# Sixteen weight chunks of a float32 decoder block: the low part built by a negative copy and an adding transfer

## The chip, the cores and the metric

The kernel runs on one core of a Trainium2 chip. The engines are TensorE (PE in the profile; its weight loads are the row PEld), VectorE (DVE), ScalarE (ACT), GpSimd (POOL) and SyncE (SP, which here issues nearly all transfers). The metric is the device time of one launch in microseconds. A span is the time from the first to the last instruction of one profiled execution.

## The reference

A decoder block on a sequence of 512 tokens of width 1024, in float32: a first gated feed-forward part, a token mixer (causal pooling beside dilated window attention, gated and merged), a second gated feed-forward part, and a final norm. The change is in the second feed-forward part only.

```python
def swiglu(u, w_in, w_out):
    a, b = jnp.split(u @ w_in, 2, axis=-1)
    return (jax.nn.silu(a) * b) @ w_out
...
u = modulate(rmsnorm(h, g_norm_ffn2[l]), sh3, sc3)
h = h + 0.5 * gt3 * swiglu(u, w_ffn2_in[l], w_ffn2_out[l])
return rmsnorm(h, g_final)
```

The hidden width is 2816, which is 22 tiles of 128.

## The kernel before, in words

**Float32 by three products.** Every float32 operand is cut into a high part of type fp32r and a low part, the rest. A product is then three matmuls into the same PSUM bank: high weight by high activation, high weight by low activation, low weight by high activation (`mm3`, lines 360 to 362; lines 745 to 747 in `product`).

**The weight pipeline.** Weights come from HBM in chunks, mostly 128x1024 float32 (512 KB), in an order that the planner `plan` writes down once (`self.order`). `fetch` issues the load of a chunk from SP (line 245) into a raw buffer as soon as one is free; three buffers are always there (`raw`), and up to four more (`X` in the profile) in part of the second feed-forward part. `split_hi` lets ScalarE copy the chunk into the ring `whi`, rounded to fp32r (line 317). `split_lo` lets VectorE subtract, wlo = raw - whi (line 329), and gives the raw buffer back; the next load into that buffer waits for this. Both rings hold 7 chunks and a little. `look(4)` asks for chunks up to four places ahead of the one in use, so TensorE's next weights are made while it works on earlier ones, and a new chunk needs ring space that TensorE has done with.

**The second feed-forward part.** The 22 hidden tiles are worked on in five parts (`PARTS`: 4, 4, 4, 4 and 6 tiles). Each part first makes hidden tiles and then runs an output part: the product of the part's hidden tiles with the matching rows of `w_out`, added into H. The first part's hidden tiles come from plain pairs (`ffn_pair`), later ones from `duo`, which saves products by a block scheme: seven products from four loaded chunks, some of them differences that VectorE makes (line 261, tiles `X` and `raw`). One product of `duo` is 24 matmuls of 256 columns; one chunk of an output part is 24 matmuls of 512 columns and feeds two banks. Each of the first four output parts uses four chunks of 128x1024 (tensor `wf2o`), and VectorE takes each bank into H (line 900). The fifth uses eight narrower ones.

**Order of the work.** Each engine runs its queue in order of the program. In an output part TensorE starts with the first chunk's high weights and asks for its low weights at the third matmul; the matmuls behind that one wait with it. The hidden tiles HI and HK for the first part's last tile come just before that part from ScalarE (line 675) and VectorE (line 676); in the first chunk their matmuls are put last. SP's loads are one queue too: a load that waits for its buffer holds all behind it.

A raw chunk can lie in the ring in two pieces, where the ring ends: the 16 chunks of the first four output parts are 14 instructions of 128x1024 and 4 of 128x512, on ScalarE and on VectorE alike.

```python
            for i, b in enumerate(bs):
                for k in range(nk if m else 0):
                    self.mm3(b, *w[nk * i + k], *hk[k], k == 0, k == nk - 1)
```

Of the kernel before, what the change touches and what calls it, by code (L numbers as in the profile page):

```python
# [11 lines left out]
AF = mybir.ActivationFunctionType  # L12
OP = mybir.AluOpType
# [5 lines left out]
KT = 8  # L19
# [107 lines left out]
PARTS = ((0, 4), (4, 8), (8, 12), (12, 16), (16, 22))  # L127
# [6 lines left out]
def pairs_before(n, part):  # L134

    k1 = PARTS[part][1]
    return k1 if part + 1 == len(PARTS) or (n == 2 and part == 0) else k1 + 2


def chunk_widths():  # L140
    outs = [D] * (KT // 2 * (len(PARTS) - 1)) + [(FT - PARTS[-1][0]) * P] * KT
    f1 = [2 * FIRST * P] * KT + [D] * (2 * (FT - FIRST)), outs
    mix = [D] * 24 + [4 * P] * 2 + ([D] * 4 + [4 * P] * 2) * (KT // 2 - 1) + [D] * KT
    return f1, mix, ([D] * (2 * FT), outs)


class Kernel:
# [6 lines left out]
    def plan(self):  # L154
        (i1, o1), mix, (i2, o2) = chunk_widths()
        self.chunks = []
        for name, ws in (("wf1i", i1), ("wf1o", o1), ("wmix", mix), ("wf2i", i2), ("wf2o", o2)):
            off, rec = 0, []
            for w in ws:
                rec.append((name, off, w))  # L160
                off += P * w
            self.chunks.append(rec)
        f1i, f1o, mx, f2i, f2o = self.chunks


        self.loads, self.order, self.last = [], [], {}
        self.shifted = set()

        def plain(recs):
            for r in recs:  # L170
                n = len(self.loads)
                self.loads.append(r)
                self.last[n] = len(self.order)
                self.order.append((r[2], n, ("raw", n), None))

        def blocks(recs):
            n = len(self.loads)
            self.shifted.update(range(len(self.order), len(self.order) + 7))
            self.loads.extend(recs)
            r11, r12, r22, r21 = (("raw", n + i) for i in range(4))  # L180
            x0, x1 = ("x", 0), ("x", 1)
            for need, src, make in ((0, r11, None), (1, x0, (x0, r12, r11)), (2, x1, (x1, r22, x0)), (3, r21, None),
                                    (3, r12, (r12, r22, r12)), (3, r22, None), (3, x0, (x0, r21, x1))):
                for j, x in enumerate((r11, r12, r22, r21)):
                    if x == src or (make and x in make):
                        self.last[n + j] = len(self.order)
                self.order.append((D, n + need, src, make))

        def shift(i):

            self.shifted.update(range(len(self.order) - i, len(self.order)))

        def ffn(n, ins, outs, first):
            j, at = first, 0
            if first:
                plain(ins[:KT])
                at = KT
            for part, (k0, k1) in enumerate(PARTS):
                while j < pairs_before(n, part):
                    if j < PLAIN[n]:  # L200
                        plain(ins[at:at + 2])
                        if n and j < 2:
                            shift(2)
                        j, at = j + 1, at + 2
                    else:
                        blocks(ins[at:at + 4])
                        j, at = j + 2, at + 4
                plain(outs[part * KT // 2:(part + 1) * KT // 2] if part + 1 < len(PARTS) else outs[-KT:])

        ffn(0, f1i, f1o, FIRST)  # L210
        shift(4)
        base = len(self.order)
        plain(mx[:26])
        for i in range(26, len(mx) - KT, 6):
            blocks(mx[i:i + 4])
            plain(mx[i + 4:i + 6])
        plain(mx[-KT:])
        self.shifted.update(range(base, base + 4))
        shift(3)
        ffn(2, f2i, f2o, 0)  # L220
        shift(5)
        self.fetched = self.done = self.made = 0

        self.ready = True
        self.pos, self.held, self.retired, self.half = 0, None, [], None

        self.small, self.smalls = None, []
        self.at, self.start, self.top = {}, {}, 0
        self.buf = {}
        self.units = {base + i: 2 * P for i in (4, 5)}  # L230
        self.units.update({base + i: T for i in range(16, 20)})
# [91 lines left out]
    def split_lo(self):  # L323

        if not self.half:
            return
        r, parts = self.half
        for y, x in parts:
            self.nc.vector.tensor_tensor(self.lo[:, y], r[:, x], self.hi[:, y], op=OP.subtract)  # L329
        i = self.done  # L330
        self.half = None
        self.done += 1
        for n in [n for n in self.buf if self.last[n] == i]:
            b = self.buf.pop(n)
            if not any(b is x for x in self.retired):
                (self.small if any(b is x for x in self.smalls) else self.free).append(b)
# [1458 lines left out]
```

## Time and profile before

| what | value |
|---|---|
| median of 3 runs | 990.43 us (990.16 to 991.58) |
| span of the profiled execution | 988.9 us, 16359 instructions |
| its time by the runs' measure | not given by itself; the median of the runs is 1.5 us above the span |
| TensorE matmul busy | 980.7 us (99%) |
| VectorE busy | 784.3 us (79%) |
| ScalarE busy | 474.7 us (48%) |
| GpSimd busy | 29.7 us (3%) |
| transfers | 141.74 MB, 143 GB/s on average |

In a row of the timeline stand the start in us, the duration in us, the engine, the line of the kernel, the operation, the tile written and the tiles read, and in brackets how long the engine sat idle before it and what ended that. In a row of the table by stretches stand the stretch with its length, and for each engine the busy time and the number of instructions, then the granted clock of TensorE, the busy share of the transfer engines and the GB/s they moved. The row of a transfer ends with the median time from issue to landing.

### The profile page before, as it was taken

The numbers are of one execution on the slowest core, as the hardware profiler recorded it, in microseconds if no ns is written. First come the engines' busy times: TensorE is split into PE (matmuls) and PEld (weight loads), VectorE is DVE, ScalarE is ACT, GpSimd is POOL, SyncE is SP. The second block draws the span as 40 slices with busy tenths as digits, with TensorE's granted clock in tenths as the row PEclk, the third lists the DMA queues.
The fourth block names the chain that finished last, engine by engine and source line by source line (L and its number), as shares of the span: only waits on it lengthen the run. The fifth ranks groups of instructions, "written<-read, shape, count | busy, mean of one in ns | idle before, by whom it ended". The sixth has DMA issues, their size and how long they took to land.

```text
span 988.9 us, 16359 instructions
## 1 busy us (share of the span) xinstructions
PE 980.7 (99%) x6688; PEld 893.3 (90%) x6688; DVE 784.3 (79%) x1090; ACT 474.7 (48%) x712; POOL 29.7 (3%) x31
## 2 busy tenths in 40 slices
PE   9999999999999999999999999999999999999997
PEld 7888999989999899888879998998899898998997
DVE  7989979889797777887878877868787776676764
ACT  5453643625435453445545552455355254352553
POOL 0000000000000000007200000000000000000002
PEclk9999999999999999999999999999999999999999
DMA  9856446465563426664233326513344134241312
GB/s 353 276 196 224 150 149 187 156 196 165 183 199 109 137 57 201 223 192 153 72 122 108 107 81 218 171 44 104 98 155 133 46 117 138 86 150 44 106 44 86
DMA packets 44876, 141.74 MB, mean 143 GB/s; under 512 B 6273, under 2 KB 9089, under 8 KB 44802
## 3 DMA queue, kind: packets, MB, share of 16 engines
q1 hardware_dynamic: 44224, 140.18, 43.9%
q8 instruction: 52, 0.85, 0.4%
q10 hardware_dynamic: 578, 0.53, 0.2%
q14 instruction: 22, 0.18, 0.1%
HBM read 135.29 MB, written 2.24 MB: 139 GB/s over the span
## 4 chain that ended last, share of the span: by engine, by line
PE 94%; DVE 2%; ACT 1%; SPq 1%; issue 1%; POOL 0%; DMA 0%; POOLq 0%; ACTq 0%; DVEq 0%
PE bank L360 15%; PE bank L361 15%; PE bank L362 15%; PE bank L746 13%; PE bank L745 13%; PE bank L747 13%; PE bank L1721 2%; PE bank L1723 1%; PE bank L1725 1%; SPq L1053 1%; PE bank L1397 1%; PE bank L1099 1%; PE bank L1150 1%; PE bank L1398 1%; PE bank L1399 1%
## 5 line engine op out<-in xcount | busy, mean ns | idle before, releaser
L329 DVE TENSOR_TENSOR wlo<-raw,whi 128x1024 fp32r<-128x1024 f32 (+4 forms) x162 | 170.6, 1066 | 52.2 <-ACT whi L317 51.9
L745 PE MATMUL bank<-UH,whi 128*128 128x256 f32 x640 | 176.7, 276 | 0.0
L746 PE MATMUL bank<-UL,whi 128*128 128x256 f32 x640 | 176.7, 276 | 0.0
L747 PE MATMUL bank<-UH,wlo 128*128 128x256 f32 x640 | 176.7, 276 | 0.0
L317 ACT ACTIVATE whi<-raw 128x1024 fp32r<-128x1024 f32 (+4 forms) x162 | 146.3, 920 | 58.4 <-DVE raw L261 55.0
L360 PE MATMUL bank<-HI,whi 128*128 128x512 f32 (+1 forms) x406 | 146.2, 360 | 0.0
L361 PE MATMUL bank<-HK,whi 128*128 128x512 f32 (+1 forms) x406 | 145.9, 359 | 0.0
L362 PE MATMUL bank<-HI,wlo 128*128 128x512 f32 (+1 forms) x406 | 145.8, 359 | 0.0
L329 DVE TENSOR_TENSOR wlo<-X,whi 128x1024 fp32r<-128x1024 f32 (+3 forms) x104 | 112.0, 1084 | 31.2 <-ACT whi L317 30.9
L745 PEld LDWEIGHTS bank<-UH,whi 128*128 128x128 f32 x640 | 120.1, 188 | 0.4
L746 PEld LDWEIGHTS bank<-UL,whi 128*128 128x128 f32 x640 | 120.2, 188 | 0.0
L747 PEld LDWEIGHTS bank<-UH,wlo 128*128 128x128 f32 x640 | 120.1, 188 | 0.0
L745 PE MATMUL bank<-SH,whi 128*128 128x256 f32 x408 | 112.7, 276 | 0.0
L746 PE MATMUL bank<-SL,whi 128*128 128x256 f32 x408 | 112.6, 276 | 0.0
L747 PE MATMUL bank<-SH,wlo 128*128 128x256 f32 x408 | 112.6, 276 | 0.0
L317 ACT ACTIVATE whi<-X 128x1024 fp32r<-128x1024 f32 (+3 forms) x104 | 95.7, 943 | 34.1 <-DVE X L261 33.4
L360 PE MATMUL bank<-UH,whi 128*128 128x512 f32 (+1 forms) x304 | 105.9, 348 | 0.0
L361 PE MATMUL bank<-UL,whi 128*128 128x512 f32 (+1 forms) x304 | 104.5, 344 | 0.1
L362 PE MATMUL bank<-UH,wlo 128*128 128x512 f32 (+1 forms) x304 | 104.2, 343 | 0.0
L362 PEld LDWEIGHTS bank<-HI,wlo 128*128 128x128 f32 x406 | 76.2, 188 | 11.7
L360 PEld LDWEIGHTS bank<-HI,whi 128*128 128x128 f32 x406 | 76.2, 188 | 11.5
L361 PEld LDWEIGHTS bank<-HK,whi 128*128 128x128 f32 x406 | 76.3, 188 | 11.3
(345 smaller groups left out, 1838.0 us busy)
## 6 DMA issues: line engine op xcount, KB each, us to landing
raw<-wmix SPq DMA_DIRECT2D x44, 512.0 KB, 3.8
raw<-wf1i SPq DMA_DIRECT2D x31, 512.0 KB, 4.7
raw<-wf2i SPq DMA_DIRECT2D x30, 512.0 KB, 3.7
ada<-wada SPq DMA_DIRECT2D x23, 512.0 KB, 5.6
AR<-wada SPq DMA_DIRECT2D x19, 512.0 KB, 4.5
X<-wf2i SPq DMA_DIRECT2D x14, 512.0 KB, 3.8
cs<-wada SPq DMA_DIRECT2D x12, 512.0 KB, 3.7
X<-wf1i SPq DMA_DIRECT2D x12, 512.0 KB, 4.3
```

What stands on the lines that cost most here:

```text
L317: self.nc.scalar.activation(self.hi[:, y], r[:, x], AF.Copy)
L329: self.nc.vector.tensor_tensor(self.lo[:, y], r[:, x], self.hi[:, y], op=OP.subtract)
L360: M(ps, hi, uh, start=start, stop=False)
L361: M(ps, hi, ul, start=False, stop=False)
L362: M(ps, lo, uh, start=False, stop=stop)
L745: M(o, hi, uh, start=start and p == 0 and k == 0, stop=False, skip_group_check=True)
L746: M(o, hi, ul, start=False, stop=False, skip_group_check=True)
L747: M(o, lo, uh, start=False, stop=k == 3, skip_group_check=True)
L1053: nc.sync.dma_start(w[32 * o:32 * o + 32], t[32 * i:32 * i + 32])
L1099: nc.tensor.matmul(S[:, o], q[:, toks], k[:, ks], start=True, stop=True, skip_group_check=True)
L1150: self.nc.tensor.matmul(self.bO[64 * h:64 * h + 64, P * hp:P * hp + P], x, pt[:, (2 * h + j) * P:(2 * h + j + 1) * P], start=j == first, s ...
L1721: M(b, hi, self.UH[k], start=k == 0, stop=False)
```

## The change

For the 16 chunks of the first four output parts of the second feed-forward part (set `added`), `split_lo` no longer subtracts on VectorE. ScalarE writes -raw, rounded to fp32r, into the place of the low part in the ring `wlo` (18 activations more: two of the chunks lie in the ring in two pieces, so there are 14 of 128x1024 and 4 of 128x512), and GpSimd issues a transfer that adds the raw chunk to what is there, from SBUF to SBUF (18 transfers). The third matmul of a chunk waits for that transfer instead of VectorE, and so does the next load into the raw buffer. The order on all queues is otherwise the same; TensorE's instructions do not change. Four output chunks of each of these parts are concerned; the fifth output part, the first feed-forward part and the mixer keep VectorE's subtraction.

```diff
-        self.shifted = set()
+        self.shifted, self.added = set(), set()
...
+                if n and part + 1 < len(PARTS):
+                    self.added.update(range(len(self.order), len(self.order) + KT // 2))
                 plain(outs[part * KT // 2:(part + 1) * KT // 2] if part + 1 < len(PARTS) else outs[-KT:])
...
         r, parts = self.half
+        i = self.done
         for y, x in parts:
-            self.nc.vector.tensor_tensor(self.lo[:, y], r[:, x], self.hi[:, y], op=OP.subtract)
-        i = self.done
+            if i in self.added:
+                self.nc.scalar.activation(self.lo[:, y], r[:, x], AF.Copy, scale=-1.0)
+                self.nc.gpsimd.dma_start(self.lo[:, y], r[:, x], accum_op=OP.add)
+            else:
+                self.nc.vector.tensor_tensor(self.lo[:, y], r[:, x], self.hi[:, y], op=OP.subtract)
```

## The prediction, made before the changed kernel was run

> **What bounds the kernel now.** I read the page's share by engine first, then the chain that ended last, then busy time by stretches of the stage that the change touches, then timelines around the four output parts.
>
> ```profile
> PE 980.7 (99%) x6688; PEld 893.3 (90%) x6688; DVE 784.3 (79%) x1090; ACT 474.7 (48%) x712; POOL 29.7 (3%) x31
> PE 94%; DVE 2%; ACT 1%; SPq 1%; issue 1%; POOL 0%; DMA 0%; POOLq 0%; ACTq 0%; DVEq 0%
> ```
>
> ```profile
> 660.00:687.00 27.00, 27.00 (x143) 23.28 (x142) 19.65 (x23) 12.19 (x18) 0.00 (x0) 1.00 0.26 78
> 687.00:709.00 22.00, 22.00 (x100) 18.23 (x99) 16.95 (x20) 7.45 (x9) 0.00 (x0) 1.00 0.36 120
> 709.00:766.00 57.00, 57.00 (x506) 57.00 (x505) 45.90 (x46) 32.41 (x43) 0.00 (x0) 1.00 0.43 137
> 766.00:788.00 22.00, 22.00 (x101) 18.24 (x100) 14.86 (x16) 6.63 (x7) 0.00 (x0) 1.00 0.17 54
> 826.00:848.00 22.00, 22.00 (x101) 18.24 (x100) 15.27 (x17) 6.72 (x8) 0.00 (x0) 1.00 0.18 58
> 886.00:908.00 22.00, 22.00 (x101) 18.24 (x100) 15.19 (x16) 6.72 (x8) 0.00 (x0) 1.00 0.19 61
> 908.00:988.00 80.00, 75.20 (x605) 72.50 (x603) 48.47 (x68) 38.18 (x63) 5.12 (x7) 1.00 0.25 80
> ```
>
> TensorE is the bound. The four output parts are the stretches that begin near 687, 766, 826 and 886 us, and through all of them TensorE is busy without a gap at a granted clock of 1.00. VectorE has room there (15 to 17 of 22 us). So time taken from VectorE buys nothing in this stage by itself; anything that makes a low weight late makes TensorE stand, and since TensorE is full until 908, what it loses there comes out at the end. The sum goes against the profiled span of 988.9 us; the median of the runs, 990.43, is 1.5 above it, and I add the same difference to it.
>
> **What is removed: VectorE's subtractions.**
>
> ```profile
> L329 DVE TENSOR_TENSOR wlo<-raw,whi 128x1024 fp32r<-128x1024 f32 x28 | 34.1, 1222 | 10.5 <-ACT whi L317 10.5
> L329 DVE TENSOR_TENSOR wlo<-X,whi 128x512 fp32r<-128x512 f32 x14 | 9.0, 687 | 3.0 <-ACT whi L317 3.0
> L317 ACT ACTIVATE whi<-raw 128x1024 fp32r<-128x1024 f32 x28 | 29.5, 1053 | 21.6 <-DVE raw L261 21.5
> L317 ACT ACTIVATE whi<-X 128x512 fp32r<-128x512 f32 x14 | 8.0, 624 | 8.2 <-DVE X L261 8.2
> ```
>
> 14 of 1.222 us and 4 of 0.687 us leave VectorE: 19.9 us. All of it lies under busy TensorE, so it is worth 0 on the path.
>
> **What is added on ScalarE.** 14 activations of 1.053 and 4 of 0.624 us: 17.2 us, about 4.3 in each part, on an engine that is busy 12 of 27 us, and 32 of 57, ahead of the parts. Here is the first part's place on ScalarE and VectorE, and TensorE's weight loads.
>
> ```profile
> 680.87 1.05 ACT L317 ACTIVATE whi<-raw 128x1024 fp32r<-128x1024 f32 x1
> 684.56 0.63 ACT L675 ACTIVATE HI<-hf 128x512 fp32r<-128x512 f32 x1 [2.65 <-DVE hf L673]
> 685.10 1.04 ACT L317 ACTIVATE whi<-raw 128x1024 fp32r<-128x1024 f32 x1
> 686.05 0.58 ACT L680 ACTIVATE u<-bank 128x512 f32<-128x512 f32 x1
> 686.52 1.05 ACT L317 ACTIVATE whi<-raw 128x1024 fp32r<-128x1024 f32 x1
> 682.71 1.22 DVE L329 TENSOR_TENSOR wlo<-raw,whi 128x1024 fp32r<-128x1024 f32 x1
> 683.84 0.68 DVE L673 TENSOR_TENSOR hf<-sl,bank 128x512 f32<-128x512 f32 x1
> 687.33 0.19 PEld L362 LDWEIGHTS bank<-HI,wlo 128*128 128x128 f32 x1
> ```
>
> The three `whi` rows are the part's first three chunks. Behind the first one ScalarE stands for 2.65 us waiting for `hf`, so the new activation fits: activations follow each other by 0.95 us (686.05 less 685.10), so it starts at 681.82 and ends at 682.87. VectorE, rid of the subtraction at 682.71, can make `hf` about 1.1 us earlier, so HI and the second chunk come earlier too, and the second added activation ends near 686.1. The silu at 686.05 and the last HI and HK are then about where they were. I cost ScalarE's work at 0; its cover is that standing time, and without it a late HI would cost up to 1.05 us once.
>
> **What is added on the path: the transfer.** Before, the first low part was there at 682.71 + 1.22 = 683.93, 3.4 us ahead of its use at 687.33. Now it is there at 682.87 + L, where L runs from the end of the activation to the landing of GpSimd's transfer. The room for L is 687.33 - 682.87 = 4.46 us. For the other parts the same rows are these (the first chunk's copy, the next ScalarE row, the load of the low weight):
>
> ```profile
> 755.97 1.05 ACT L317 ACTIVATE whi<-raw 128x1024 fp32r<-128x1024 f32 x1
> 758.19 0.60 ACT L767 ACTIVATE sl<-bank 128x512 f32<-128x512 f32 x1 [1.17 <-PE bank L747]
> 766.33 0.19 PEld L362 LDWEIGHTS bank<-HI,wlo 128*128 128x128 f32 x1
> 815.96 1.05 ACT L317 ACTIVATE whi<-raw 128x1024 fp32r<-128x1024 f32 x1
> 826.32 0.19 PEld L362 LDWEIGHTS bank<-HI,wlo 128*128 128x128 f32 x1
> 876.22 1.05 ACT L317 ACTIVATE whi<-X 128x1024 fp32r<-128x1024 f32 x1
> 886.30 0.19 PEld L362 LDWEIGHTS bank<-HI,wlo 128*128 128x128 f32 x1
> ```
>
> With 2.00 us from the start of the copy to the end of the added activation, the room is 766.33 - 757.97 = 8.36, 826.32 - 817.96 = 8.36 and 886.30 - 878.22 = 8.08 us. The idle 1.17 us ahead of `sl` takes the added activation there.
>
> L is not in this trace: GpSimd issues no transfer in it. The nearest rows are SP's loads of 512 KB from HBM in this stage (first line below) and SP's copies of 64 KB within SBUF (second line, with one row of their issue).
>
> ```profile
> DMA to landing us min/median/max: 3.4/3.7/6.2
> DMA to landing us min/median/max: 1.9/2.0/4.3
> L1053 SPq DMA_DIRECT2D rt<-rt x16: 512/582/1580, 402.6 to 446.4; - x16
> ```
>
> From below: no added transfer of 512 KB should land sooner than the fastest load, 3.4 us. From above: it reads source and destination, so as long as two of the slowest loads one after the other, 12.4 us. In between: load and small copy differ by 1.7 us for 448 KB, which is 1.94 us for 512 KB; read twice that is 3.9; with the 2.0 us that even the small copy takes, and 1.6 us for the issue by an engine that has not issued one yet (the longest issue row; the usual 0.58 would make L 6.5), L = 7.5 us. I take 7.5, an estimate from these rows; it lies nearest to twice a median load, 7.4.
>
> Then the first part's TensorE stands 7.5 - 4.46 = 3.0 us, and the matmuls behind the third one with it. Parts two to four have 8.1 to 8.4 us of room: 0. Later chunks of a part are needed 5.5 us after one another (22 us over four chunks) and copied at most 4.2 us after one another (685.10 less 680.87), so they gain room, as long as a transfer holds the transfer engines for less than 5.5 us (3.9 by the estimate). The stage's transfer share of 0.17 to 0.43 leaves room for the 16 x 0.5 MB, read twice and written once.
>
> **What is moved in SP's queue.** A raw buffer now comes free at the landing, not at VectorE's end, some 6 us later, and every load behind it in SP's queue waits too. The tightest is the first part's fourth chunk, which loads into the first one's buffer: issued at 682.87 + 7.5 = 690.4, landed 3.7 later, 2.0 on ScalarE, 7.5 to add: 703.6. Three chunks of 5.5 us on from 687.33, and 3.0 later, TensorE asks for it at 706.8. Behind it, the load of the next stage's third chunk is issued at 703.6, lands at 707.3, and with three more steps of about 1.2 us (difference, copy, subtraction) is ready at 710.9; TensorE asks for it two products after 709 + 3.0, at 717.4 (2.71 us each: 21 products fill the 57 us from 709 on). This too I cost at 0; with L left open it is ready at 695.9 + 2L and wanted at 710.0 + L, so it begins to cost from L = 14. VectorE's taking of a finished bank waits behind the next chunk's subtraction in its queue, and that bank is wanted two chunks, 11 us, later: 0.
>
> GpSimd's queue holds nothing else until the end of the kernel: no wait of these 18 stands ahead of other work.
>
> Sum: 0 (VectorE) + 0 (ScalarE) + 3.0 (first transfer) + 0 (later ones, loads) = 988.9 + 3.0 = 991.9 us of span, 993.5 us by the runs.
>
> The Trainium skill, "DMA: Bandwidth & Descriptors", section on the anatomy of one DMA on the SWDGE path, gives a transfer issued by GpSimd about 2.0 us plus its bytes at 436 GB/s, which is an estimate of 3.2 us for 512 KB, or 4.4 us with the bytes counted twice. No run here shows it. By that rule L would stay within the room even of the first part, and the sum would be 990.4 us, no change; my sum goes by the rows, and this outcome is the first rival.
>
> **The rivals.** *The transfer is hidden (not slower).* L is at most 4.46 us, so even the first part's low weight is in time. For it: the fastest load takes 3.4 us and a small copy 2.0. Against it: the median load alone takes 3.7, without a second read or GpSimd's issue. It decides at L = 4.46; the time is 988.9 + 0, 990.4 by the runs.
>
> *All four parts stand.* L is over 8.4: TensorE waits at the head of each part. At the upper end of 12.4 that is 7.9 + 4.0 + 4.0 + 4.3 = 20.2 us, so 1010.6; at 10 us it is 5.5 + 1.6 + 1.6 + 1.9 = 10.6, so 1001.0. For it: L is unseen, and GpSimd issues its first transfer in the tightest place. Against it: two median loads are 7.4 us.
>
> *VectorE's relief pays (faster).* 19.9 us less on the second busiest engine bring forward something TensorE waits for. TensorE has idle time after 660 only in the last stretch, 80.0 - 75.2 = 4.8 us, and no removed subtraction lies later than about 885 us. Half of it would give 988.0; I see no way there.
>
> **How the numbers follow.** Chances: first part alone stands (L from 4.46 to 8.4, 0 to 4 us lost) 0.50; hidden 0.13; all four 0.33; faster 0.04. A change under 0.2%, 2.0 us, is about what a measurement can't tell from none. L up to 6.5 loses under 2.0 us: that is the hidden case and 0.20 out of the first. So faster 0.04, same 0.33, slower 0.63. Predicted is the likeliest case with L = 7.5: 993.5. The range reaches from no loss (990.4, and 0.6 below it for the runs' spread) to L = 12.4: 989.8 to 1010; the likeliest case alone is 990.4 to 994.4.
>
> **What would show it.** In the changed kernel's waits TensorE or its weight loads should wait for the transfer into `wlo`, once near 687 us, for about 3.0 us, and not near 766, 826 and 886 (then the room of 8 us holds). The row of transfers by GpSimd shows L nearly directly. VectorE's busy time falls by about 20 us and ScalarE's rises by about 17. Wrong would be: a wait at the heads of all four parts (L over 8.4), none at all (L under 4.5), a wait for a load from HBM in the next `duo` (the buffers), or longer activations or matmuls beside the new transfers.

## The result and the profile after

| | before | after |
|---|---|---|
| median of the runs | 990.39 us (990.16 to 991.58) | 995.1 us (993.53 to 996.17) |
| ratio, with its 95% interval | | 1.0046 (1.0034 to 1.0059) |
| profiled execution: time and span | span 988.9 us | 996.17 us, span 994.0 us |

The changed kernel is slower by 4.7 us at the medians; 993.5 was forecast. The profiled execution of the changed kernel is the slowest of its four. Its page has, by engine, the busy time, and then the chain that ended last:

```profile
PE 983.2 (99%) x6688; PEld 894.6 (90%) x6688; DVE 765.0 (77%) x1072; ACT 490.7 (49%) x730; POOL 45.6 (5%) x49
PE 89%; DVE 3%; issue 3%; DMA 3%; SPq 1%; ACT 1%; POOL 0%; POOLq 0%; DVEq 0%; ACTq 0%
```

VectorE's busy time fell by 19.3 us and ScalarE's rose by 16.0, as forecast (20 and 17). In the chain TensorE's share falls from 94% to 89%, and 3% of DMA is new. The table by stretches of the changed kernel (columns as before) says in which stage TensorE stood:

```profile
687.00:709.00 22.00, 21.70 (x96) 17.65 (x95) 6.82 (x8) 6.19 (x8) 1.73 (x3) 1.00 0.84 214
709.00:766.00 57.00, 55.83 (x472) 55.04 (x471) 47.16 (x49) 35.67 (x48) 1.70 (x2) 1.00 0.41 122
766.00:788.00 22.00, 22.00 (x116) 18.95 (x116) 13.55 (x16) 9.24 (x11) 2.65 (x4) 1.00 0.76 192
```

From 687 to 908 us only the first of the four output parts, and the `duo` behind it, have time in which TensorE is idle. The transfer engines' share in the four output parts was 0.17 to 0.36 and is now 0.74 to 0.84. The waits of the changed kernel from 686 to 726 us name the places. A row says who waited, then behind the arrow what ended the wait, then us in all, times, longest:

```profile
PEld bank L372 <- ACT whi L319: 1.4, 1, 1.4
PE bank L372 <- DVE H L906: 1.0, 1, 1.0
PEld bank L368 <- DMA wlo<-raw: 0.7, 1, 0.7
PE bank L368 <- DMA wlo<-raw: 0.3, 1, 0.3
PEld bank L751 <- ACT bank L758: 0.3, 1, 0.3
PEld bank L751 <- ACT u L758: 0.2, 1, 0.2
```

(The changed kernel's lines are six further down than before: 362 is 368, 745 is 751, 900 is 906; line 372 is the short matmul at the head of a `duo`.) One wait is the forecast one, for the transfer, but it is 0.7 us and not 3.0. The largest stands at line 372 and wasn't in the sum. Its first row names ScalarE's copy `whi`, but the chunk of this matmul, the first of the `duo`, was copied from 697.98 to 699.04; what came last is in the second row, VectorE's work on H at line 906. Where these fall is seen in the timeline of TensorE's matmuls in the changed kernel:

```profile
687.84 0.50 PE L368 MATMUL bank<-HI,wlo 128*128 128x512 f32 x1 [0.30 <-DMA wlo<-raw]
...
709.07 0.39 PE L368 MATMUL bank<-HI,wlo 128*128 128x512 f32 x1
710.49 0.35 PE L372 MATMUL bank<-UH,whi 128*128 128x240 f32 x1 [1.03 <-DVE H L906]
```

A matmul of 512 columns is followed by the next after 0.23 us; from 709.07 to 710.49 it took 1.42, a loss of 1.2 us.

**The whole account.** The first load of a low weight in an output part is a good mark, since it is the same instruction in every kernel. Before, the first two parts' marks are at 687.33 and 766.33 and the fourth's at 886.30. In the changed kernel TensorE's weight loads have them here:

```profile
687.84 0.19 PEld L368 LDWEIGHTS bank<-HI,wlo 128*128 128x128 f32 x1 [0.72 <-DMA wlo<-raw]
...
770.54 0.19 PEld L368 LDWEIGHTS bank<-HI,wlo 128*128 128x128 f32 x1
...
890.51 0.19 PEld L368 LDWEIGHTS bank<-HI,wlo 128*128 128x128 f32 x1
```

The last mark is the activation of ScalarE that ends the final norm, before and after:

```profile
983.53 0.38 ACT L632 ACTIVATE AR<-bank 128x256 f32<-128x256 f32 x1 [1.05 <-PE bank L458]
```

```profile
987.75 0.38 ACT L638 ACTIVATE AR<-bank 128x256 f32<-128x256 f32 x1 [1.05 <-PE bank L464]
```

| from one mark to the next | before | after | more |
|---|---|---|---|
| start to the first part's mark | 687.33 | 687.84 | 0.51 |
| to the second part's | 79.00 | 82.70 | 3.70 |
| to the fourth's | 119.97 | 119.97 | 0 |
| to the final norm | 97.23 | 97.24 | 0 |
| to the end of the span | 5.37 | 6.25 | 0.88 |
| span | 988.9 | 994.0 | 5.1 |

So the loss lies in the forecast wait, in something between the first and the second output part (3.7), and at the end of the program (0.9). Parts two to four cost nothing. The first row, 0.51, is not the wait by itself, which is 0.6 us by the matmuls' starts. The first 256-column matmul ahead of this part starts at 623.5 us before and at 623.9 in the changed kernel, so its execution was some 0.5 us later ahead of all that was changed. Against that, the profile before is 0.6 us slower between 636 and 665 us: 152 of its steps from one 256-column matmul to the next take 118 ns there, and only 23 in the changed kernel's, where most others take 113.

**The 3.7 us.** Three pieces make it up: 1.3 us at 709 (the wait, and 0.1 in the matmul behind it); two short waits near 716 and 722 at line 751, with 0.3 to 0.4 us each by the matmuls' starts; and then the matmuls of 256 columns come more slowly. Here are the first and the twentieth of twenty that follow each other, before, and in the changed kernel:

```profile
742.75 0.28 PE L746 MATMUL bank<-UL,whi 128*128 128x256 f32 x1
...
744.90 0.28 PE L747 MATMUL bank<-UH,wlo 128*128 128x256 f32 x1
```

```profile
742.75 0.28 PE L751 MATMUL bank<-SH,whi 128*128 128x256 f32 x1
...
744.98 0.28 PE L752 MATMUL bank<-UL,whi 128*128 128x256 f32 x1
```

Nineteen steps take 2.15 us before, 113 ns each, and 2.23 us after, 117 ns each, at the same granted clock of 1.00 and with no wait in the rows. Over longer stretches the two steps are 113.3 and 117.8 ns. From 722 to 770 us 407 steps are slow ones: 1.8 us. The sum 1.3 + 0.7 + 1.8 = 3.8 is 0.1 above the 3.7 of the marks.

**How the wait at 709 comes about.** The chain of the changed kernel from 683 to 711 us, without its matmuls:

```profile
683.07 4.73 DMA wlo<-raw
...
695.90 7.27 DMA wlo<-raw
...
703.24 3.99 DMA raw<-wf2i
...
707.33 1.23 DVE X L263
...
```

The fourth chunk's load waited for the first chunk's transfer, so its own transfer began at 695.90, and took 7.27 us beside two loads and the end of the third chunk's transfer. SP's next load waited for that until 703.2 and landed at 707.2. (Of the four tiles called X two take loads; the other two hold the differences.) VectorE's queue shows who stood behind that load:

```profile
701.66 1.22 DVE L263 TENSOR_TENSOR X<-raw,raw 128x1024 f32<-128x1024 f32 x1
707.33 1.23 DVE L263 TENSOR_TENSOR X<-raw,X 128x1024 f32<-128x1024 f32 x1 [4.44 <-DMA raw<-wf2i]
708.47 1.22 DVE L336 TENSOR_TENSOR wlo<-X,whi 128x1024 fp32r<-128x1024 f32 x1
709.60 1.40 DVE L906 SCALAR_TENSOR_TENSOR H<-bank,mod,H 128x512 f32<-128x512 f32 x2
```

The difference for a later product stood for 4.44 us, and behind it in the queue stood the taking of two banks into H (line 906), which TensorE needed at 709.3 for the next `duo`. The first of the two ends near 710.35, and the matmul of line 372 starts at 710.49. Before, the same difference waited for its load for 0.24 us, and these two banks were taken 11 us sooner:

```profile
696.13 1.22 DVE L261 TENSOR_TENSOR X<-raw,X 128x1024 f32<-128x1024 f32 x1 [0.24 <-DMA raw<-wf2i]
...
698.41 1.40 DVE L900 SCALAR_TENSOR_TENSOR H<-bank,mod,H 128x512 f32<-128x512 f32 x2
```

The two short waits near 716 and 722 come from the same backlog. VectorE has no pause from 707.33 to 725, its next difference is late too, and ScalarE's copy of the chunk made of it waits for it. The copy of a bank that TensorE wants at 716.1 stands behind that in ScalarE's queue and ends at 716.3:

```profile
714.77 1.06 ACT L319 ACTIVATE whi<-raw 128x1024 fp32r<-128x1024 f32 x1 [3.87 <-DVE raw L263]
715.74 0.58 ACT L758 ACTIVATE bank<-bank 128x512 f32<-128x512 f32 x1
```

### The profile page after: what moved, and what is told of

Read it like the earlier page. It is cut to its first block, busy times and chain, and to the rows that moved or that the text cites. A ratio compares the mean times of both kernels' runs of the same rounds, so it can differ in the third digit from the quotient of the medians.

```text
span 994.0 us, 16420 instructions
## 1 busy us (share of the span) xinstructions
PE 983.2 (99%) x6688; PEld 894.6 (90%) x6688; DVE 765.0 (77%) x1072; ACT 490.7 (49%) x730; POOL 45.6 (5%) x49
## 4 chain that ended last, share of the span: by engine, by line
PE 89%; DVE 3%; issue 3%; DMA 3%; SPq 1%; ACT 1%; POOL 0%; POOLq 0%; DVEq 0%; ACTq 0%
PE bank L366 14%; PE bank L368 14%; PE bank L367 14%; PE bank L751 13%; PE bank L753 12%; PE bank L752 12%; PE bank L1727 2%; PE bank L1729 1%; PE bank L1731 1%; DMA wlo<-raw 1%; SPq L1059 1%; PE bank L1403 1%; PE bank L1105 1%; PE bank L1156 1%; PE bank L1404 1%
## 5 line engine op out<-in xcount | busy, mean ns | idle before, releaser
L336 DVE TENSOR_TENSOR wlo<-raw,whi 128x1024 fp32r<-128x1024 f32 (+4 forms) x148 | 155.6, 1064 | 53.9 <-ACT whi L319 53.6
L336 DVE TENSOR_TENSOR wlo<-X,whi 128x1024 fp32r<-128x1024 f32 (+3 forms) x100 | 106.8, 1077 | 22.8 <-ACT whi L319 22.3
```

## The experiments

All ratios are to the kernel before on the same chip, whose median was 990.2 to 990.4 in every set. The theory after the result: the loss belongs to the first output part alone, by the first chunk's transfer (the wait at 687) and the fourth chunk's (the wait at 709). Its rivals: every part costs something through the busier transfer engines, or ScalarE's added activations cost.

**Parts two to four alone.**

```diff
-                if n and part + 1 < len(PARTS):
+                if n and 0 < part < len(PARTS) - 1:
```

> Only output parts two to four (12 chunks) go by ScalarE and GpSimd's transfer; the first part keeps VectorE's subtraction. Theory A, all of the loss comes out of the first part (a late first low weight, and loads held by the adding transfers): 990.4 us, within 0.7 us of before, and no wait of TensorE between 687 and 726 us. Rival B, the transfers or ScalarE's extra work cost something in every part: about three quarters of the 4.7 us remain, 993.9 us.

Measured: 990.94 us, ratio 1.0005 (0.9996 to 1.0013). The weight loads at the first two marks:

```profile
686.49 0.19 PEld L368 LDWEIGHTS bank<-HI,wlo 128*128 128x128 f32 x1
...
765.49 0.19 PEld L368 LDWEIGHTS bank<-HI,wlo 128*128 128x128 f32 x1
```

79.00 us lie between them, as before. In this kernel the added transfers took up to 10.2 us to land, and no TensorE wait came of it: the room of 8 us at the heads is not all that the later chunks have.

**Part one alone.**

```diff
-                if n and part + 1 < len(PARTS):
+                if n and part == 0:
```

> Only the first output part (4 chunks) is changed. Theory A: the whole loss is there with 4 of the 16 chunks, 993 to 996 us, as with all of them. Rival B: about a quarter of the loss, 991.6 us.

Measured: 993.48 us, ratio 1.0031 (1.002 to 1.0042). Its waits from 684 to 726 us are those of the changed kernel, the one at the `duo` shorter:

```profile
PEld bank L372 <- ACT whi L319: 0.8, 1, 0.8
PEld bank L368 <- DMA wlo<-raw: 0.7, 1, 0.7
PE bank L372 <- DVE H L906: 0.4, 1, 0.4
```

The two runs together put the stalls into the first part.

**The first chunk's low part back on VectorE** (part one; the other 15 chunks as changed).

```diff
-                    self.added.update(range(len(self.order), len(self.order) + KT // 2))
+                    self.added.update(range(len(self.order) + (part == 0), len(self.order) + KT // 2))
```

> As the change, but the first output part's first chunk goes back to VectorE's subtraction (15 chunks stay changed). Theory A: its low weight is in time and the fourth chunk's load, which takes the first chunk's buffer, is issued near 684 us and not 688, so the fourth chunk's transfer ends some 4 to 5 us earlier and the later stall near 709 us goes too: 990.4 to 991.0 us. Rival A2, only the late first low weight goes and the stall near 709 us stays, because the fourth chunk's own transfer is what holds the next load: 993.5 to 994.5 us.

Measured: 992.5 us, ratio 1.0021 (1.0011 to 1.0031); the expectation was too low. The runs fall into two groups, 991.5 to 991.9 and 993.1 to 994.8, and the profiled one (993.2) belongs to the second. Both waits are gone from its table. Its marks:

```profile
686.39 0.19 PEld L368 LDWEIGHTS bank<-HI,wlo 128*128 128x128 f32 x1
...
767.59 0.19 PEld L368 LDWEIGHTS bank<-HI,wlo 128*128 128x128 f32 x1
```

81.20 us instead of 79.00, without a listed wait of 0.2 us or more: here the step of the 256-column matmuls is 117.8 ns from 713.5 on, behind a single step of 162 ns at 713.48, where ScalarE's copy of a bank was late. A hiccup of 49 ns stands ahead of a loss of 2.0 us (453 slow steps).

**The fourth chunk's low part back on VectorE** (part one).

```diff
-                    self.added.update(range(len(self.order), len(self.order) + KT // 2))
+                    self.added.update(range(len(self.order), len(self.order) + KT // 2 - (part == 0)))
```

> As the change, but the first output part's fourth chunk goes back to VectorE's subtraction. Theory A: the wait for the first low weight near 687 us stays (0.7 to 0.9 us), the one near 709 us goes, since the next load into that buffer is released some 6 us earlier, and with it the slower pace of the 256-column matmuls from 716 to 770 us: 991.3 us. Rival: the first wait alone leads to the slower pace, or the near-709 stall comes from the fourth chunk's late load alone: 993 us or more.

Measured: 991.79 us, ratio 1.0012 (1.0004 to 1.0021). The wait at 687 is there, the one at 709 is not:

```profile
687.63 0.19 PEld L368 LDWEIGHTS bank<-HI,wlo 128*128 128x128 f32 x1 [0.71 <-DMA wlo<-raw]
...
766.55 0.19 PEld L368 LDWEIGHTS bank<-HI,wlo 128*128 128x128 f32 x1
```

78.92 us between them. So the wait at 709 hangs on the fourth chunk's transfer, by way of the loads behind it, and without it the step stays at 113 ns too. (With only the first chunk back the fourth has its transfer, but that begins at 691.28 and not at 695.90, and the wait is gone too.)

**Both the first and the fourth chunk back** (part one).

```diff
-                    self.added.update(range(len(self.order), len(self.order) + KT // 2))
+                    self.added.update(range(len(self.order) + (part == 0), len(self.order) + KT // 2 - (part == 0)))
```

> As the change, but the first output part's first and fourth chunk go back to VectorE's subtraction (14 chunks stay changed). If the loss is the first chunk's late low weight and the chain of two adding transfers through one raw buffer, nothing is left: no wait of TensorE from 687 to 726 us, quick pace, 990.4 to 991.0 us. If any adding transfer in the first part costs: 991.5 us or more.

Measured: 991.61 us, ratio 1.0013 (1.0004 to 1.0023), 0.6 us above what was expected. TensorE loses nothing: its marks stand at 686.55, 765.56 and 885.53 us, 79.01 and 119.97 apart. What is left lies at the end. The final norm's activation:

```profile
982.76 0.38 ACT L638 ACTIVATE AR<-bank 128x256 f32<-128x256 f32 x1 [1.05 <-PE bank L464]
```

From there to the end of the span of 989.4 us it is 6.6 us, against 5.37 before.

**What ScalarE's activations cost.** VectorE adds the chunk to the negative copy; GpSimd transfers nothing.

```diff
-                self.nc.gpsimd.dma_start(self.lo[:, y], r[:, x], accum_op=OP.add)
+                self.nc.vector.tensor_tensor(self.lo[:, y], r[:, x], self.lo[:, y], op=OP.add)
```

> ScalarE's part alone: it writes the negative high part into the low part's place for the 16 chunks, and VectorE adds the chunk to it instead of GpSimd's transfer. Theory A (ScalarE's 17 us lie beside other work): 990.4 us, within 0.7. Rival (the extra activations in ScalarE's queue delay what TensorE waits for): over 991.5 us.

Measured: 992.59 us, ratio 1.0024 (1.0015 to 1.0034), where no change was expected. Its waits from 684 to 726 us:

```profile
DVE wlo L334 <- ACT wlo L333: 3.6, 3, 1.2
...
PEld bank L366 <- ACT HI L681: 1.3, 1, 1.3
...
PE bank L366 <- ACT HI L681: 0.9, 1, 0.9
PEld bank L367 <- DVE HK L682: 0.5, 1, 0.5
```

HI is late when ScalarE has its added activations and VectorE isn't relieved: the first two marks are 80.73 us apart, 1.7 more than before, at the quick step. This is more than the added activations alone: VectorE's adds wait for the negative copies (first row), so it makes the input of the last HI at 690.60 and not at 688.75 as before. In the changed kernel VectorE, rid of its subtraction, makes that input at 687.20, and HI is in time. That the activations would cost without this relief is likely, but no run has them without either the relief or VectorE's longer wait.

**A plain transfer in place of the adding one** (it leaves out the add: the low part is then the chunk itself).

```diff
-                self.nc.gpsimd.dma_start(self.lo[:, y], r[:, x], accum_op=OP.add)
+                self.nc.gpsimd.dma_start(self.lo[:, y], r[:, x])
```

> The changed kernel with a plain copy in the place of the adding transfer (the low part is then the chunk itself, so the computed values are not the reference's). It prices the second read. If the addition's second read costs as my working had it (1.9 us for 512 KB), the landing of an undisturbed 512 KB transfer falls from 4.7 to about 3 us and the median from about 6 to 4.5; if issue and completion dominate, it stays within 0.7 us of 4.7.

Measured: 991.66 us in one run; no wait of TensorE. Landing of the transfers, and then the first one's issue on GpSimd:

```profile
DMA to landing us min/median/max: 2.9/4.1/6.3
```

```profile
682.95 0.75 POOL L334 DMA_DIRECT2D wlo<-raw  x1 [205.83 <-ACT wlo L333]
```

The adding transfer of the changed kernel, by the row of its line and GpSimd's timeline (four of the 14 in this row are of 256 KB; the landings are those of all 18):

```profile
L334 POOL DMA_DIRECT2D wlo<-raw x14: 852/861/1117, 683.1 to 890.1; - x14
DMA to landing us min/median/max: 4.5/5.6/10.0
```

```profile
683.07 1.04 POOL L334 DMA_DIRECT2D wlo<-raw  x1 [205.81 <-ACT wlo L333]
```

The add costs 1.6 us in the quickest transfer of 512 KB (4.5 less 2.9), and GpSimd's own instruction is 0.3 us longer with it.

**Where the two steps of the 256-column matmuls come from.** Four kernels tried whether the short matmul at the head of a `duo` (240 columns, line 372; its first operand `extra`) sets the step. Two theories: it selects the step by its being there at the head, or the step changes at each odd break in the stream. In the kernel before, without it in the second feed-forward part:

```diff
-                    self.duo(n, j, last, tail and j + 2 == FT, extra)
+                    self.duo(n, j, last, tail and j + 2 == FT, extra and not n)
```

> The kernel before, without the one extra 240-column matmul (function settle) that stands ahead of each run of 256-column products in the second feed-forward part; its result is overwritten anyway. It asks whether these products have two paces without any added transfer. Pace theory (the pace of the 256-column matmuls depends on how the run of them starts, 113.3 or 117.8 ns each): some or all runs go at 117.8 ns, which is up to 4.5 ns for each of about 1900 matmuls, 2 to 9 us: 992.4 to 999 us. Rival (the slower pace of the changed kernel comes from the transfers' traffic): 990.0 us, all at 113.3 ns.

Measured: 996.44 us, ratio 1.0063 (1.0051 to 1.0076). Its matmuls:

```profile
742.81 0.28 PE L746 MATMUL bank<-UL,whi 128*128 128x256 f32 x1
...
744.93 0.28 PE L746 MATMUL bank<-UL,whi 128*128 128x256 f32 x1
```

18 steps in 2.12 us, 118 ns, with no transfer by GpSimd in the kernel and no wait: the slow step doesn't need the added transfers. In the changed kernel, with a short matmul ahead of each `duo` and not only of the first of a stage:

```diff
-                    self.duo(n, j, last, tail and j + 2 == FT, extra)
+                    self.duo(n, j, last, tail and j + 2 == FT, extra or n)
```

> The changed kernel, with that extra 240-column matmul ahead of every block of seven products in the second feed-forward part (five more of them, about 0.1 us each). Pace theory: the waits near 687, 709, 716 and 722 us stay, but the second block of the stage after the first output part, near 730 us, starts anew at 113.3 ns, so some 1.4 us less than the changed kernel where that is in the slow pace: 992.5 to 993.8 us. Rival (traffic): the pace stays 117.8 ns, 995.5 us.

Measured: 997.86 us, ratio 1.0072 (1.0058 to 1.0086), the opposite of what was expected: one in the middle of a run of 256-column matmuls takes the run to the slow step, and in stage one the next brought it back. In the kernel before, with two short matmuls at the head, and with three:

```diff
-        if extra:
+        for _ in range(extra):
...
-                    self.duo(n, j, last, tail and j + 2 == FT, extra)
+                    self.duo(n, j, last, tail and j + 2 == FT, 2 * extra if n else extra)
```

> The kernel before, with the extra 240-column matmul issued twice instead of once ahead of each of the four runs of 256-column products in the second feed-forward part; no added transfer anywhere. Toggle theory (each such odd-sized start, like each short wait, takes the 256-column matmuls to the other of two paces): two of them bring back the slow pace of none, 117.8 ns throughout, 996.5 us. Rival (any settling matmul sets the quick pace): 113.3 ns, 990.7 us.

> The same with three of them. Toggle theory: quick again, 113.3 ns, 990.6 to 991.2 us (eight matmuls of about 0.1 us more). Rival, that more of them only add disorder: 117.8 ns, 996.5 us or more.

Measured: 990.9 us, ratio 1.0007 (0.9998 to 1.0016), and 991.27, ratio 1.001 (1.0001 to 1.0019); the step is 113.3 ns in both. So at the head of these runs one, two or three of them all give the quick step, and none the slow one: it isn't that every short matmul turns it over. What turns it in the middle of a run stays open.

**The changed kernel again.**

> The change once more, for more runs. Theory: 0.9 us near 687, some 1.2 near 709, 0.5 in two short waits, and 1.7 us more in those runs in which these waits leave the 256-column matmuls in the slow pace until 770 us: runs at about 993.5 to 994.3 and at about 995.5 to 996.2, median between 993.5 and 996.2 us. Rival (one state and noise): one cluster around 995 us.

Measured: 993.84 us (992.3 to 995.69), ratio 1.0036 (1.0024 to 1.0049). The five runs are spread over this range and don't form the two groups that were expected. The profiled run is the quickest, 992.3, below both:

```profile
687.75 0.19 PEld L368 LDWEIGHTS bank<-HI,wlo 128*128 128x128 f32 x1 [0.71 <-DMA wlo<-raw]
...
766.71 0.19 PEld L368 LDWEIGHTS bank<-HI,wlo 128*128 128x128 f32 x1
```

78.96 us between the marks. VectorE's queue in this execution:

```profile
705.01 1.23 DVE L263 TENSOR_TENSOR X<-raw,X 128x1024 f32<-128x1024 f32 x1 [1.42 <-DMA raw<-wf2i]
...
707.29 1.40 DVE L906 SCALAR_TENSOR_TENSOR H<-bank,mod,H 128x512 f32<-128x512 f32 x2
```

The fourth chunk's transfer began at 695.90 as in the first profile, but took 5.2 us and not 7.27; why is not shown. So the late load came 2.3 us sooner (705.01 instead of 707.33), both banks were taken by 708.7, and there is neither the wait at 709 nor those at 716 and 722 nor the slow step. These together are what separates this execution from the one of 996.17: 3.7 us in the marks, 3.8 in the spans (994.0 and 990.2).

## Why the prediction was nearly right, and where it was not

The direction and the size came out (993.5 forecast, 995.1 and in a second set 993.84 measured), but not by the forecast sum. The sum had one term, a wait of 3.0 us; that wait measured 0.6, and four things that the sum had at nothing make up the rest: the wait at 709, the two short waits behind it, the slower step and the end of the program. That the total came so near is luck.

- **TensorE is the bound, and what it loses comes out at the end:** right. The 3.7 us lost by 766 stand unchanged at the final norm.
- **VectorE's subtractions are worth 0:** right as far as the parts go: with them gone from parts two to four alone the time is unchanged (1.0005). What they may be worth is the cover for ScalarE, below.
- **ScalarE's activations cost 0, up to 1.05 us once without their cover:** the 0 is right. With VectorE adding in place of the transfer, HI came late and TensorE lost 1.7 us, but there VectorE also waited for ScalarE, so the 1.05 was not tried by itself.
- **The first transfer, L = 7.5 us against 4.46 of room:** the mechanism and its place were right, the size was not. The activation ended at 682.74 (681.69 + 1.05), the transfer landed at 687.80 (683.07 + 4.73): L = 5.1. The wait is 0.7 us of the weight load, 0.6 by the matmuls' starts, instead of 3.0. Both parts of the estimate were too high: 1.04 us for the issue, not 1.6, and 3.7 from its end to the landing, not 5.9; 0.3 us between the activation and the issue had no term. The rule of the Trainium skill ("DMA: Bandwidth & Descriptors", anatomy of one DMA on the SWDGE path) with the bytes counted twice gave 4.4 us; the quickest adding transfer took 4.5, and 2.9 without the add, where the rule gives 3.2. For a transfer that little else disturbs the trace agrees. In the output parts, where the transfer engines are 0.74 to 0.84 busy, an adding transfer took up to 10.0 us, which the rule doesn't give.
- **Parts two to four, 0:** right, even with landings of up to 10 us.
- **The queue of SP and the taking of banks, 0:** this is the step that failed. The late loads were followed to the product that needs the chunk (wanted at 717.4), and the banks' takings were held up by a subtraction of 1.2 us only. But VectorE works in order: the difference that waits for the late load stands ahead of the takings, so the banks were late as long as the load was, and TensorE wants them at 709.3, 8 us before the chunk. The late load itself came when it was forecast (issued at 703.24 and landed at 707.23; forecast 703.6 and 707.3), and what the prediction named as a sign of being wrong, a wait for a load in the next `duo`, is what VectorE then did for 4.44 us. The condition "begins to cost from L = 14" was that of the wrong user.

  For the banks the same sum begins to cost from about L = 9, an estimate: by the prediction's terms the late load lands at 692.3 + 2L, the first bank is taken 3.1 us later (707.23 to 710.35 here), at 695.4 + 2L, and it is wanted at 708.86, where the `duo` began before, + L - 4.46. So the right user would still have given 0 at L = 7.5, since the forecast wait of 3.0 us would have put off TensorE as well. The other half of the error is one L for all transfers: the first took 4.73 us, which held TensorE up little, and the fourth 7.27. The wait at 709 cost 1.3 us in one execution, with 0.7 us in the two short waits behind it, and 0 in another, in which the fourth transfer took 5.2.
- **Not in the sum at all:** the slower step of the 256-column matmuls (1.8 us, in some executions), and the end of the program (0.3 to 1.3 us).

Of the rivals, a faster kernel is excluded, and all four parts standing (no wait at 766, 826 or 886), and so is the hidden transfer: the weight load waited 0.7 us at 687 in every profile that has the first chunk's adding transfer.

## What to carry to other kernels

When a transfer is put in place of an engine's operation, follow the buffer that it gives back later: the load that waits for it, the engine whose queue stands for that load, and everything else in that queue, then compare with the earliest thing wanted out of it, not with the late chunk's own use. An edit on two engines can be free only because one half relieves the other; try the halves apart. A loss of 0.1% to 0.5% can vary between executions by as much as its size, so read it from marks in several profiles, not from one.

## What the runs showed that was not expected

- Matmuls of 256 columns come at one of two steps, 113.3 or 117.8 ns, for a whole run of them, at the same granted clock. One short matmul at the head of a `duo` run gives the quick one, none the slow one (990.4 against 996.4 us for the kernel), and a hiccup of 49 ns or a short matmul in the middle stands ahead of a change to the slow one. The run of 256-column matmuls from 648 to 665 us, which has no short matmul at its head in any kernel, is slow in the profile before and quick in the other profiles, so the head alone doesn't decide. The cause is open. The Trainium skill ("TensorE: Matmul & The Clock Gate", back-to-back issue gap) gives for 256 columns only the gap of an isolated matmul, 262 cycles at 2.4 GHz, which is an estimate of 109 ns; both steps here, in streams with a weight load for each matmul, are longer.
- From the final norm's activation to the end of the span it is 5.3 to 5.4 us in the kernel before and those made from it, and 5.7 to 6.6 us in all made from the changed one, 5.9 even in that without transfers by GpSimd, though the change touches nothing there. It makes most of the 1.2 us that remain when TensorE loses nothing. Another 0.35 us of the loss lies outside the span: the runs' time is 2.15 us above the span in the changed kernel and 1.8 in the kernel before. Why was not settled for either.
